# Second mixer: the rotation taken from the projection itself, head scales applied last; a fourth chunk by seven products in the last down projection

## The chip, the cores and the metric

The program runs on one core of one Trainium2 chip. The metric is the device time of one execution in microseconds (us). The kernel before has a median of 954.87 us over three executions (954.74 to 955.77).

A core has five instruction streams that run beside one another and meet through semaphores. PE (TensorE) multiplies matrices, and loads its stationary operand in instructions of their own (PEld). DVE (VectorE) and ACT (ScalarE) work element by element and can read the matrix results in PSUM. POOL (GpSimd) works element by element, on SBUF. SP (SyncE) issues most of the transfers. Each stream is executed in the order in which the program was written.

## The reference, cut to what matters

Two layers, each with two half-step feed-forward networks around a mixer. Sequence 256, width 1024, all in float32.

```python
for i in range(DEPTH):
    h = rmsnorm(x, ffn1_norm[i])
    x = x + 0.5 * swiglu(h, ffn1_w_gate[i], ffn1_w_up[i], ffn1_w_down[i])
    h = rmsnorm(x, mix_norm[i])
    q_s, k_s, v_s, q_m = jnp.split(h @ w_in[i], [768, 1536, 2304], axis=-1)
    ...                                   # memory attention o_m, both layers
    if i % 2 == 0:
        ...                               # first mixer: chunked attention with a bias
    else:                                 # second mixer
        q = rmsnorm(q_s.reshape(B, S, 6, 2, 64), b_q_norm[j])
        k = rmsnorm(k_s.reshape(B, S, 6, 2, 64), b_k_norm[j])
        q = apply_rope(q, cos, sin)
        k = apply_rope(k, cos, sin)
        ...                               # differential attention o_s
    x = x + jnp.concatenate([o_s, o_m], axis=-1) @ w_out[i]
    h = rmsnorm(x, ffn2_norm[i])
    x = x + 0.5 * swiglu(h, ffn2_w_gate[i], ffn2_w_up[i], ffn2_w_down[i])
```

`apply_rope` turns the two halves of each head of 64 by an angle: `[x1 cos - x2 sin, x2 cos + x1 sin]`. The norm multiplies a head by one number, and the rotation is linear, so the two can change places as long as the gains of the norm are folded into the tables of cosines and sines, which they are.

## The kernel before

**Products in three.** Every matrix product of weights and activations is taken in float32 by splitting both sides into a high part (rounded to the type fp32r) and a low part, the rest. `dense` (L504) issues three matmuls of 128x512 for one block: high times high (L511), high times low weights (L514), low activations times high weights (L517). One block is 128 rows of a weight matrix by 512 columns.

**Weights.** All weights stream through once. A "chunk" is 1 MB of weights, four blocks. `loader` brings chunks into three buffers `raw`, over SP's queue. `split_hi` (ACT, L338) casts each block to `hi`, and `split_lo` (DVE, L356) subtracts to get `lo`. Four buffers of `hi` and four of `lo` hold split chunks. A raw buffer is free again when the last `lo` of its chunk is done, and a split buffer when PE has used it.

**Chunks by seven.** In a down projection a chunk has a 2x2 form: two halves of the inner dimension and two of the columns, and the two token blocks make it two by two on the other side as well. A plain chunk takes 8 blocks of PE (`down`, four weight blocks for two token blocks each). A chunk by seven (`seven_item`, `seven_forms`, `seven`, `seven_sums`) takes 7, in the manner of Strassen and Winograd: it makes four sums of weight blocks (`wsum`, L350), splits seven blocks instead of four, makes four sums of activation blocks (`sf`, L681), splits those as well (L690, L694), and gathers four of its products in PSUM banks `m`, which `seven_sums` adds to the result once, behind the last such chunk. `SEVEN` (L377) lists for each feed-forward network which of the 11 chunks go by seven. The first of a list takes two split buffers. The others are "guests": one split buffer, and for the blocks 4 to 6 the tiles `xh` and `xl` of the activations, which are idle during the down projection (`gxh`, `gxl`). Only one guest can be in them: `xt_room` is set at the start of the down projection and again when PE has used a guest up, and the next guest is not split before. The activation side of the third and later chunk of a list waits until PE has reached the second chunk of the list (`prog[0] >= sv[1]`). The last three chunks, 8 to 10, come last for each quarter of the result.

**The order.** All streams are written in one order, made when the program is built. `Flow` (L47) is a small clock: each step says how long it takes on its engine (`flow.act`, `flow.dve`, `flow.pool`), and each thread of work, a Python generator, is resumed when the clock says that what it waits for is done. PE's stream is the backbone; work of other threads is put between its blocks when the clock has it ready. A step that takes longer on the chip than its line says is therefore put too early in PE's stream, and PE waits for it there.

**The second mixer.** `proj` runs five projections: heads 0 to 3 of q and k, v, then the two other groups of q and k, and the rest of v with the memory's q. `qk_evac` takes each result `pj` (128 tokens by 512, 8 heads) through `head_norm`: square on ACT (L916), sum by head on DVE (L919), scale and add on DVE (L530) and power -1/2 on POOL (L532), then the product of the result and both scales on DVE (L925, `qkn`). Then the rotation: two products with the sines on POOL (L1259), one with the cosines on DVE (L1262), their sum on DVE (L1266). Then four transposes on PE (`qktp`, L525), and copies to `qk`, `k` and `q`. There are six such chains, three groups by two token blocks. `attn_diff` follows for each. ACT also copies attention weights out of PSUM (L1374), and `of` (L1512) is a scale of the attention's own norm, which also has a power on POOL.

Of the kernel before, what the change touches and what calls it, by code (L numbers as in the profile page):

```python
# [12 lines left out]
F32 = mybir.dt.float32  # L13
# [3 lines left out]
AF = mybir.ActivationFunctionType  # L17
ALU = mybir.AluOpType
AX = mybir.AxisListType

P = 128
# [3 lines left out]
HD = 64  # L25
# [3 lines left out]
EPS = 1e-6  # L29
# [113 lines left out]
def kernel(  # L143
# [10 lines left out]
    nc = tc.nc  # L154
    PSUM = bass.MemoryType.PSUM
    NRAW, NHL, NT2 = 3, 4, 19
    flow = Flow()
# [11 lines left out]
    banks = Slots(flow, pp, "ps", 8)  # L169
    g4 = Slots(flow, gp, "g", 12)  # L170
    g2 = Slots(flow, t2, "t", NT2)
    ctx.enter_context(tc.manual_schedule())

    def small(shape, name):
        return sm.tile(shape, F32, tag="s", name=name)
# [18 lines left out]
    nhalf = const.tile([P, 8], F32, name="nhalf")  # L194
# [179 lines left out]
    def rows2(w, r):  # L374
        return [(lambda raw: k2(raw), w[r * 256:(r + 1) * 256, :].rearrange("(k p) n -> p k n", p=P))]

    SEVEN = {(0, 1): (), (0, 2): (1, 4, 7), (1, 1): (1, 4, 7), (1, 2): (1, 4, 7)}  # L377
    PAIR = {(0, 1): 4, (0, 2): 3, (1, 1): 3, (1, 2): 3}

    def turned2(w, r):  # L380
# [147 lines left out]
    def rsqrt(dst, ss, n, scale):  # L528
        v = small([P, 8], "v")
        nc.vector.tensor_scalar(out=v[:, :n], in0=ss, scalar1=scale, scalar2=EPS, op0=ALU.mult, op1=ALU.add)  # L530
        yield flow.dve(n)
        nc.gpsimd.tensor_tensor(out=dst, in0=v[:, :n], in1=nhalf[:, :n], op=ALU.pow)  # L532
        yield flow.pool(0.3 + 0.165 * n)


    class Xt:
# [81 lines left out]
    def ffn(l, nm, xt, gc_next):  # L618
        hts = [None] * NG
        htt = [None] * NG  # L620
        sv = SEVEN[l, nm]
        prog = [-1]
# [290 lines left out]
    def head_norm(ps, nh, rstd, name):  # L913
        yield g2.has(4)
        sq = g2.take([P, nh * HD], F32, "sq")
        nc.scalar.activation(sq, ps, AF.Square, scale=rstd)  # L916
        yield flow.act(nh * HD)
        ss = small([P, 8], "hss")
        nc.vector.tensor_reduce(out=ss[:, :nh], in_=sq.rearrange("p (h d) -> p h d", d=HD), axis=AX.X, op=ALU.add)  # L919
        g2.give()  # L920
        flow.dve(nh * HD)
        f = small([P, 8], "hf")
        yield from rsqrt(f[:, :nh], ss[:, :nh], nh, 1.0 / HD)
        nat = g2.take([P, nh * HD], F32, name)
        nc.vector.scalar_tensor_tensor(out=nat.rearrange("p (h d) -> p h d", d=HD),  # L925
                                       in0=ps.rearrange("p (h d) -> p h d", d=HD), scalar=rstd,
                                       in1=f[:, :nh].unsqueeze(2).broadcast_to([P, nh, HD]),
                                       op0=ALU.mult, op1=ALU.mult)
        yield flow.dve(nh * HD, 0.06)
        return nat  # L930
# [160 lines left out]
    ropeC = const.tile([P, 2, 2, HD], F32, name="ropeC")  # L1091
    ropeS = const.tile([P, 2, 2, HD], F32, name="ropeS")
# [109 lines left out]
    def mixer(l, xt, gc_next):  # L1202
        typ_a = l % 2 == 0
# [33 lines left out]
        class Heads:  # L1237
            def __init__(self):
                self.t = [None, None]
                self.k = None  # L1240

        def qk_evac(c):
            def run(ps, tb, t):
                qk = qkt.setdefault(c, Heads())
                yield t
                yield lambda: xt.rt[tb] is not None
                nat = yield from head_norm(ps, 8, xt.r[tb], "qkn")
                banks.give()
                if not typ_a:
                    yield g2.has(2)  # L1250
                    n4 = nat.rearrange("p (j h d) -> p j h d", j=2, h=4)
                    m2 = g2.take([P, 512], F32, "m2")
                    m1 = g2.take([P, 512], F32, "m1")
                    m1v = m1.rearrange("p (j h d) -> p j h d", j=2, h=4)
                    m2v = m2.rearrange("p (j h d) -> p j h d", j=2, h=4)
                    for hf in range(2):
                        own = slice(hf * 32, hf * 32 + 32)
                        oth = slice(32 - hf * 32, 64 - hf * 32)
                        nc.gpsimd.tensor_tensor(  # L1259
                            out=m2v[:, :, :, own], in0=n4[:, :, :, oth],  # L1260
                            in1=ropeS[:, tb, :, own].unsqueeze(2).broadcast_to([P, 2, 4, 32]), op=ALU.mult)
                    nc.vector.tensor_tensor(out=m1v, in0=n4,  # L1262
                                            in1=ropeC[:, tb].unsqueeze(2).broadcast_to([P, 2, 4, HD]), op=ALU.mult)
                    flow.dve(512)
                    yield flow.pool(1.4)
                    nc.vector.tensor_add(m1, m1, m2)  # L1266
                    g2.give(2)
                    nat = m1
                    yield flow.dve(512)
                yield banks.has()  # L1270
                tp = bank("qktp")
                for j in range(4):
                    t = turn(tp[:, j, :], nat[:, j * P:(j + 1) * P], typ_a and j < 2)
                g2.give()
                yield t
                gq, gk = (gcs[:, 2:3], gcol[:, GC_AK:GC_AK + 1]) if typ_a else (None, None)
                ts_ = slice(tb * P, (tb + 1) * P)
                yield lambda: g2.left > 0 and (g4.left > 0 if tb == 0 else qk.k is not None)
                if tb == 0:
                    qk.k = g4.take([P, 2, 2, SEQ], F32R, f"k{c}")  # L1280
                    qk.f = f = g2.take([P, 2, 2, P], F32, f"qk{c}")
                    if typ_a:
                        nc.scalar.activation(f[:, 0], tp[:, 0:2, :], AF.Copy, scale=gq)
                        nc.scalar.activation(f[:, 1], tp[:, 2:4, :], AF.Copy, scale=gk)
                        flow.act(256)
                        t = flow.act(256)
                    else:
                        nc.scalar.copy(out=f.rearrange("p a b c -> p (a b) c"), in_=tp)
                        t = flow.act(512)
                    banks.give()  # L1290
                    yield t
                    nc.scalar.copy(out=qk.k[:, 0, :, ts_], in_=f[:, 1])
                    yield flow.act(256)
                    nc.vector.tensor_sub(qk.k[:, 1, :, ts_], f[:, 1], qk.k[:, 0, :, ts_].bitcast(F32))
                    flow.dve(256)
                else:
                    qk.q = g2.take([P, 2, 2, P], F32R, f"q{c}")
                    yield from split_evac((qk.k[:, 0, :, ts_], qk.k[:, 1, :, ts_]), tp[:, 2:4, :], gk)
                    t = yield from split_evac((qk.q[:, 0], qk.q[:, 1]), tp[:, 0:2, :], gq)
                    banks.give()  # L1300
                qk.t[tb] = t
            return run
# [308 lines left out]
        for tb in range(2):  # L1611
            flow.spawn(finish(acc, tb, nxt, gc_next, False))
            for hf in range(2):
                for i in range(2, 4):
                    for k in range(2):
                        t = outp(i, k, tb, hf)
# [10 lines left out]
    xt = Xt(PAIR[0, 1] is not None)  # L1627
# [34 lines left out]
    for l in range(DEPTH):  # L1662
        xt = ffn(l, 1, xt, GC_MIX + l * KT)
        xt = mixer(l, xt, GC_FFN2 + l * KT)
        xt = ffn(l, 2, xt, None if l == DEPTH - 1 else GC_FFN1 + (l + 1) * KT)
# [53 lines left out]
```

## Time and profile before

| | us |
|---|---|
| median of three executions | 954.87 |
| the profiled execution, whole | 955.69 |
| its span, first to last instruction | 953.9 |
| PE busy | 945.6 |
| DVE busy | 820.0 |
| ACT busy | 587.0 |
| POOL busy | 109.1 |

The profile counts a matmul as busy from start to end, and matmuls overlap: one of 128x512 is shown as 0.39 us long, and the next starts after 0.23 us. What a matmul costs is therefore read from the distance of the starts. The granted clock of PE is full all through the execution. The second mixer lies between about 670 and 765 us of the span; the last down projection lies between 892 and 950 us.

### The profile page before, as it was taken

The page shows a single profiled execution, that of the slowest core. Times are in us where ns is not written, and L with a number is a line of the kernel's source. Part 1 is how long each engine was busy: PE and PEld are TensorE (multiplying, and loading weights), DVE is VectorE, ACT ScalarE, POOL GpSimd, SP SyncE. Part 2 cuts the span into 40 slices and gives each one's busy share as a digit, 9 for nine tenths or more (in the row PEclk, how much of TensorE's full clock was granted, in tenths as well). Part 3 has the DMA queues.
Part 4 walks back from the last instruction along what each step waited for, and adds up shares of the span by engine and source line. Part 5 has one row for each costly group of instructions (what it writes and reads, how often), then busy time and mean ns, then how long its engine had stood idle before and what let it go on. Part 6 is the DMA issues. An engine that isn't in the chain of part 4 may idle for free.

```text
span 953.9 us, 13334 instructions
## 1 busy us (share of the span) xinstructions
PE 945.6 (99%) x4475; PEld 774.1 (81%) x4475; DVE 820.0 (86%) x1483; ACT 587.0 (62%) x1121; POOL 109.1 (11%) x160
## 2 busy tenths in 40 slices
PE   9999999999999999999999999999999999999998
PEld 7888888887777888888888888888787778888886
DVE  7898978888777899979889899796999888999884
ACT  6556566677676746647546656564676865665650
POOL 1000057621210100000000000000434200000000
PEclk9999999999999999999999999999999999999999
DMA  8987799486525387887746679775641367588751
GB/s 265 289 263 236 224 354 296 158 276 210 177 90 177 97 266 225 262 287 219 245 146 219 208 226 288 247 253 166 196 158 57 121 214 228 183 275 276 239 197 45
DMA packets 169887, 204.04 MB, mean 214 GB/s; under 512 B 10137, under 2 KB 145114, under 8 KB 169818
## 3 DMA queue, kind: packets, MB, share of 16 engines
q1 hardware_dynamic: 169498, 202.78, 66.0%
q8 instruction: 35, 0.57, 0.3%
q10 hardware_dynamic: 320, 0.40, 0.1%
q14 instruction: 34, 0.28, 0.1%
HBM read 188.99 MB, written 14.16 MB: 213 GB/s over the span
## 4 chain that ended last, share of the span: by engine, by line
PE 90%; DVE 6%; DMA 2%; ACT 1%; issue 1%; SPq 0%; ACTq 0%; DVEq 0%
PE gu L517 13%; PE gu L514 13%; PE gu L511 13%; PE acc L511 9%; PE acc L517 9%; PE acc L514 9%; PE pair_m L511 3%; PE pair_m L514 3%; PE pair_m L517 3%; PE pj L517 2%; PE pj L511 2%; PE pj L514 2%; DVE lo L356 2%; PE S L1360 1%; DMA x<-in_x_dram 1%; PE AV L1441 1%
## 5 line engine op out<-in xcount | busy, mean ns | idle before, releaser
L338 ACT CAST hi<-raw 128x512 fp32r<-128x512 f32 (+1 forms) x467 | 336.3, 770 | 172.6 <-DMA raw<-in_ffn_w_up_dram 45.6
L356 DVE TENSOR_TENSOR lo<-raw,hi 128x512 fp32r<-128x512 f32 (+1 forms) x467 | 391.9, 875 | 35.5 <-ACT hi L338 35.4
L514 PE MATMUL gu<-lo,xh 128*128 128x512 f32 x576 | 224.7, 390 | 0.5 <-DVE lo L356 0.5
L517 PE MATMUL gu<-hi,xl 128*128 128x512 f32 x576 | 224.5, 390 | 0.4 <-DVE xl L562 0.4
L511 PE MATMUL gu<-hi,xh 128*128 128x512 f32 x576 | 224.4, 390 | 0.0
L517 PEld LDWEIGHTS gu<-hi,xl 128*128 128x128 f32 x576 | 108.1, 188 | 23.9 <-DVE xl L562 1.7
L514 PEld LDWEIGHTS gu<-lo,xh 128*128 128x128 f32 x576 | 108.1, 188 | 23.5 <-DVE lo L356 1.4
L511 PEld LDWEIGHTS gu<-hi,xh 128*128 128x128 f32 x576 | 108.2, 188 | 22.3
L517 PE MATMUL acc<-hi,ht 128*128 128x512 f32 x280 | 109.5, 391 | 0.0
L511 PE MATMUL acc<-hi,ht 128*128 128x512 f32 x280 | 109.2, 390 | 0.0
L514 PE MATMUL acc<-lo,ht 128*128 128x512 f32 x280 | 109.1, 390 | 0.0
L338 ACT CAST hi<-wsum 128x512 fp32r<-128x512 f32 x82 | 47.7, 619 | 26.5 <-DVE wsum L350 26.5
L514 PE MATMUL pj<-lo,xh 128*128 128x512 f32 x160 | 64.0, 400 | 0.0
L517 PE MATMUL pj<-hi,xl 128*128 128x512 f32 x160 | 63.8, 399 | 0.0
L511 PE MATMUL pj<-hi,xh 128*128 128x512 f32 x160 | 63.8, 399 | 0.0
L514 PEld LDWEIGHTS acc<-lo,ht 128*128 128x128 f32 x280 | 52.6, 188 | 10.9
L517 PEld LDWEIGHTS acc<-hi,ht 128*128 128x128 f32 x280 | 52.6, 188 | 10.8
L511 PEld LDWEIGHTS acc<-hi,ht 128*128 128x128 f32 x280 | 52.6, 188 | 10.7
L532 POOL TENSOR_TENSOR xr<-v,nhalf 128x1 f32<-128x1 f32 x12 | 10.3, 861 | 435.1 <-DVE v L530 435.1
L356 DVE TENSOR_TENSOR lo<-wsum,hi 128x512 fp32r<-128x512 f32 x82 | 52.8, 680 | 0.0
L633 ACT ACTIVATE sil<-gu,xr 128x256 f32<-128x256 f32 x72 | 33.7, 468 | 29.8 <-PE gu L517 29.7
L532 POOL TENSOR_TENSOR hf<-v,nhalf 128x8 f32<-128x8 f32 (+1 forms) x20 | 31.4, 1570 | 87.3 <-DVE v L530 78.9
(232 smaller groups left out, 1429.5 us busy)
## 6 DMA issues: line engine op xcount, KB each, us to landing
raw<-in_ffn_w_down_dram SPq DMA_DIRECT2D x176, 256.0 KB, 4.5
raw<-in_ffn_w_gate_dram SPq DMA_DIRECT2D x82, 512.0 KB, 4.0
raw<-in_ffn_w_up_dram SPq DMA_DIRECT2D x82, 512.0 KB, 5.4
raw<-in_w_in_dram SPq DMA_DIRECT2D x32, 512.0 KB, 4.4
hd<-hb SPq DMA_DIRECT2D x44, 256.0 KB, 4.6
hr<-hd SPq DMA_DIRECT2D x44, 256.0 KB, 4.6
raw<-in_w_out_dram SPq DMA_DIRECT2D x8, 1024.0 KB, 5.1
raw<-in_w_mem_kv_dram SPq DMA_DIRECT2D x4, 1024.0 KB, 5.3
```

The source lines that it names most:

```text
L338: nc.scalar.copy(out=it.part(0, q, w), in_=src())
L356: nc.vector.tensor_sub(it.part(1, q, w), src(), it.part(0, q, w).bitcast(F32))
L511: nc.tensor.matmul(out=ps, lhsT=xh, rhs=wh, start=start, stop=False)
L514: nc.tensor.matmul(out=ps, lhsT=xh, rhs=wl, start=False, stop=False)
L517: nc.tensor.matmul(out=ps, lhsT=xl, rhs=wh, start=False, stop=stop)
L532: nc.gpsimd.tensor_tensor(out=dst, in0=v[:, :n], in1=nhalf[:, :n], op=ALU.pow)
L633: nc.scalar.activation(sil, ps[tb][:, 0:256], AF.Silu, scale=xt.r[tb])
L1360: nc.tensor.matmul(out=ss[e][:, pr, :nk], lhsT=q[rows, pr, :], rhs=k[rows, pr, :], start=i == 0, stop=i == len(passes) - 1)
L1441: nc.tensor.matmul(out=av[64 * e:64 * e + 64, pr, :], lhsT=vsrc(kb, pr, e), rhs=pts[e][:, pr, kb, :], start=(kb == 0), stop=(kb == nb - 1))
```

## The change

There are three edits.

1. In the second mixer the rotation no longer waits for the norm. A copy of the projection goes to SBUF on ACT (`own`), ahead of the square. DVE multiplies the projection in PSUM by the cosines, after which the PSUM bank is given back; POOL multiplies the copy by the sines, the two halves crossed. The sum of squares and its power run beside that, with the power behind the two products in POOL's stream. DVE adds the two products, and a last DVE step multiplies by the token's scale and the head's scale. The first mixer keeps `head_norm`.
2. The clock's lines: the power on POOL is taken as 0.5 + 0.17 n us for n columns in place of 0.3 + 0.165 n, everywhere (`rsqrt`); the two products on POOL as 2.1 us in place of 1.4, and the power inside the new function as 1.9 us.
3. In the last down projection the chunks by seven are 1, 3, 5 and 7 in place of 1, 4 and 7.

```diff
-    SEVEN = {(0, 1): (), (0, 2): (1, 4, 7), (1, 1): (1, 4, 7), (1, 2): (1, 4, 7)}
+    SEVEN = {(0, 1): (), (0, 2): (1, 4, 7), (1, 1): (1, 4, 7), (1, 2): (1, 3, 5, 7)}
...
         nc.gpsimd.tensor_tensor(out=dst, in0=v[:, :n], in1=nhalf[:, :n], op=ALU.pow)
-        yield flow.pool(0.3 + 0.165 * n)
+        yield flow.pool(0.5 + 0.17 * n)
...
+        def rotated(ps, tb, rstd):
+
+            heads = lambda t: t.rearrange("p (j h d) -> p j h d", j=2, h=4)
+            yield g2.has(4)
+            own, sq, m1, m2 = (g2.take([P, 512], F32, n) for n in ("qko", "sq", "m1", "m2"))
+            nc.scalar.copy(out=own, in_=ps)
+            ta = flow.act(512)
+            nc.scalar.activation(sq, ps, AF.Square, scale=rstd)
+            ts = flow.act(512)
+            nc.vector.tensor_tensor(out=heads(m1), in0=heads(ps),
+                                    in1=ropeC[:, tb].unsqueeze(2).broadcast_to([P, 2, 4, HD]), op=ALU.mult)
+            t = flow.dve(512)
+            banks.give()
+            yield ta
+            for hf in range(2):
+                to = slice(hf * 32, hf * 32 + 32)
+                src = slice(32 - hf * 32, 64 - hf * 32)
+                nc.gpsimd.tensor_tensor(out=heads(m2)[:, :, :, to], in0=heads(own)[:, :, :, src],
+                                        in1=ropeS[:, tb, :, to].unsqueeze(2).broadcast_to([P, 2, 4, 32]), op=ALU.mult)
+            tm = flow.pool(2.1)
+            yield max(t, ts)
+            ss = small([P, 8], "hss")
+            nc.vector.tensor_reduce(out=ss, in_=sq.rearrange("p (h d) -> p h d", d=HD), axis=AX.X, op=ALU.add)
+            g2.give()
+            flow.dve(512)
+            f, v = small([P, 8], "hf"), small([P, 8], "v")
+            nc.vector.tensor_scalar(out=v, in0=ss, scalar1=1.0 / HD, scalar2=EPS, op0=ALU.mult, op1=ALU.add)
+            yield flow.dve(8)
+            nc.gpsimd.tensor_tensor(out=f, in0=v, in1=nhalf, op=ALU.pow)
+            tf = flow.pool(1.9)
+            yield tm
+            nc.vector.tensor_add(m1, m1, m2)
+            g2.give(2)
+            flow.dve(512)
+            yield tf
+            by_head = lambda t: t.rearrange("p (h d) -> p h d", d=HD)
+            nc.vector.scalar_tensor_tensor(out=by_head(m1), in0=by_head(m1), scalar=rstd,
+                                           in1=f.unsqueeze(2).broadcast_to([P, 8, HD]), op0=ALU.mult, op1=ALU.mult)
+            yield flow.dve(512, 0.1)
+            return m1
...
-                nat = yield from head_norm(ps, 8, xt.r[tb], "qkn")
-                banks.give()
-                if not typ_a:
-                    yield g2.has(2)
-                    n4 = nat.rearrange("p (j h d) -> p j h d", j=2, h=4)
-                    m2 = g2.take([P, 512], F32, "m2")
-                    m1 = g2.take([P, 512], F32, "m1")
...
-                    for hf in range(2):
...
-                        nc.gpsimd.tensor_tensor(
-                            out=m2v[:, :, :, own], in0=n4[:, :, :, oth],
-                            in1=ropeS[:, tb, :, own].unsqueeze(2).broadcast_to([P, 2, 4, 32]), op=ALU.mult)
-                    nc.vector.tensor_tensor(out=m1v, in0=n4,
-                                            in1=ropeC[:, tb].unsqueeze(2).broadcast_to([P, 2, 4, HD]), op=ALU.mult)
-                    flow.dve(512)
-                    yield flow.pool(1.4)
-                    nc.vector.tensor_add(m1, m1, m2)
-                    g2.give(2)
-                    nat = m1
-                    yield flow.dve(512)
+                if typ_a:
+                    nat = yield from head_norm(ps, 8, xt.r[tb], "qkn")
+                    banks.give()
+                else:
+                    nat = yield from rotated(ps, tb, xt.r[tb])
```

## What was predicted

> **What bounds the kernel now.** I read the page first: the busy shares and the chain of waits.
>
> ```profile
> span 953.9 us, 13334 instructions
> ...
> PE 945.6 (99%) x4475; PEld 774.1 (81%) x4475; DVE 820.0 (86%) x1483; ACT 587.0 (62%) x1121; POOL 109.1 (11%) x160
> ...
> PE 90%; DVE 6%; DMA 2%; ACT 1%; issue 1%; SPq 0%; ACTq 0%; DVEq 0%
> ```
>
> PE is never idle for long. So time goes down in two ways only: fewer matmuls, or shorter gaps between them. The second view, PE's waits from 660 to 790 us, holds the second mixer and the entry of the last feed-forward network; the third gives the stages' busy time.
>
> ```profile
> PE qktp L525 <- DVE m L1266: 0.7, 2, 0.6
> PE otp L525 <- DVE of L1512: 0.5, 1, 0.5
> PE AV L1498 <- ACT PT L1374: 0.5, 1, 0.5
> PE gu L517 <- DVE xl L562: 0.4, 1, 0.4
> ```
> ```profile
> 670.00:760.00 90.00, 88.03 (x487) 69.78 (x487) 82.60 (x184) 64.60 (x180) 32.60 (x27) 1.00 0.42 137
> 893.00:932.00 39.00, 39.00 (x174) 32.30 (x173) 35.19 (x64) 25.20 (x49) 0.00 (x0) 1.00 0.61 200
> ```
>
> The columns of the last two rows are the stretch, its length, then busy us of PE, PEld, DVE, ACT and POOL, the granted clock (1.00) and DMA. In the mixer all of PE's waits make 0.7 + 0.5 + 0.5 = 1.7 us, and the entry behind it 0.4. Only the first row, 0.7 us, belongs to the rotation. DVE is the next engine, 82.6 of 90 us, but it mostly runs ahead of PE. In the last down projection PE has no gap at all, so there only a smaller number of matmuls helps.
>
> **The fourth chunk by seven.** One block less is three matmuls less. What they cost is the distance of starts, since each is shown as 0.39 us and overlaps the next:
>
> ```profile
> 914.02 0.39 PE L511 MATMUL acc<-hi,h 128*128 128x512 f32 x1
> 914.25 0.39 PE L514 MATMUL acc<-lo,h 128*128 128x512 f32 x1
> 914.47 0.39 PE L517 MATMUL acc<-hi,h 128*128 128x512 f32 x1
> 914.70 0.39 PE L511 MATMUL acc<-hi,h 128*128 128x512 f32 x1
> ```
>
> From 914.02 to 914.70 is 0.68 us for three. **-0.68 us**, if the blocks arrive in time. What is added is DVE and ACT work, and these rows price it:
>
> ```profile
> 898.60 2.50 DVE L356 TENSOR_TENSOR lo<-raw,hi 128x512 fp32r<-128x512 f32 x4 [0.77 <-ACT hi L338]
> ...
> 902.34 0.68 DVE L350 TENSOR_TENSOR wsum<-raw 128x512 f32<-128x512 f32 x1
> 902.94 0.68 DVE L350 TENSOR_TENSOR wsum<-raw,wsum 128x512 f32<-128x512 f32 x1
> ...
> 913.18 0.28 DVE L681 TENSOR_TENSOR sf<-hr 128x128 f32<-128x128 f32 x1
> ...
> 914.11 0.69 DVE L350 TENSOR_TENSOR wsum<-raw 128x512 f32<-128x512 f32 x1
> ...
> 929.88 2.50 DVE L356 TENSOR_TENSOR lo<-raw,hi 128x512 fp32r<-128x512 f32 x4 [2.94 <-ACT hi L338]
> ```
>
> A step of 512 columns starts 0.60 us behind the one before. Three more `lo` (1.8), four `wsum` (2.4) and four `sf` (913.18 to 914.11, 0.93), and `lo` of the activations in three pieces in place of one, which I estimate from the same rows at +0.5: DVE gets 5.6 us more. It has 39.0 - 35.2 = 3.8 us idle there, nearly all of it the two waits of 0.77 and 2.94 us for `hi`. So 1.8 us don't fit and eat the lead. How large is the lead? Chunk 10's four `lo` end at 929.88 + 2.50 = 932.4. The last part begins where the guest ends:
>
> ```profile
> 933.06 0.39 PE L511 MATMUL acc<-gxh,h 128*128 128x512 f32 x1
> ...
> 933.74 0.39 PE L511 MATMUL acc<-hi,ht 128*128 128x512 f32 x1
> ```
>
> Chunk 10 is the fifth block from 933.74, at 933.74 + 4 x 0.68 = 936.5. The lead is 4 us; with 1.8 us of overload and PE 0.68 us earlier 1.5 are left. The guests follow closer (5 behind 3, 7 behind 5, one plain chunk of 8 x 0.68 = 5.5 us between). A guest's blocks 4 to 6 need three casts and three `lo` behind its forerunner's end, under 4 us, and are used 5.5 + 4 x 0.68 = 8.2 us behind it: covered. ACT gets about 2.3 us (three casts and two small steps) and is busy 25 of 39. Transfers don't grow: SP brings the same chunks, and three raw buffers free later by up to the 1.8 us. If the cover fails, PE waits for a `lo`: up to 1.8 us, so this edit lies between -0.7 and +1.1. I take -0.68, since every lead found is larger than the overload.
>
> **The rotation.** What each chain uses now, from the grouped rows:
>
> ```profile
> L916 ACT ACTIVATE sq<-pj,xr 128x512 f32<-128x512 f32 x12 | 8.3, 688 | 1.6 <-PE pj L517 1.5
> L925 DVE SCALAR_TENSOR_TENSOR qkn<-pj,xr,hf 128x512 f32<-128x512 f32 x12 | 8.9, 744 | 0.3 <-POOL hf L532 0.3
> L1374 ACT COPY PT<-ptp 128x512 f32<-128x512 f32 x17 | 9.8, 584 | 3.6 <-PE ptp L525 3.4
> L1259 POOL TENSOR_TENSOR m<-qkn,ropeS 128x256 f32<-128x256 f32 x12 | 12.1, 1027 | 7.5 <-DVE qkn L925 4.7 <-ACT k L1022 1.8 <-PE pj L517 1.1
> L532 POOL TENSOR_TENSOR hf<-v,nhalf 128x8 f32<-128x8 f32 x6 | 11.0, 1832 | 17.4 <-DVE v L530 9.1 <-DVE sst L583 8.3
> ```
>
> DVE: sum, scale, two products, one addition before; the same five after, so I put DVE at 0 (one product changes from SBUF to PSUM input, the head scales the other way). ACT: six copies more, 6 x 0.58 = 3.5 us, hidden in ACT's 25 us of idle time. POOL: the same instructions. PE: the same.
>
> The chain in length: before, square 0.69, sum 0.69, scale 0.17, power 1.83, product 0.74, two POOL products 2.05, addition 0.68: 6.9 us without queues. After: copy 0.58, POOL products 2.05, power 1.83 behind them, last product 0.74 (as L925, its nearest row; 0.68 as other DVE steps at least): 5.2 us; the branch through square and sum is done earlier. 1.7 us shorter, but PE has other blocks meanwhile, so the length itself is worth nothing. What counts is whether the clock's places fit.
>
> ```profile
> 685.19 0.39 PE L517 MATMUL pj<-hi,xl 128*128 128x512 f32 x1
> 686.15 0.63 PE L525 MATMUL qktp<-ident,m 128*128 128x128 f32 x4 [0.57 <-DVE m L1266]
> ...
> 691.24 0.63 PE L525 MATMUL qktp<-ident,m 128*128 128x128 f32 x4 [0.16 <-DVE m L1266]
> ```
>
> These are the two waits for the rotated result. The clock's 1.4 us for POOL's products stands against 2.05 measured, and 0.3 + 0.165 x 8 = 1.62 for the power against 1.83: 0.64 us too early in all, the size of the larger wait. The new lines, 2.1 and 1.9, fit. So I take these **-0.7 us** as gained. The wait for `of` has the same reason (0.63 on the clock for n = 2, 0.84 after the change); I credit half of its 0.5, **-0.2**. The other waits I leave as they are: the first mixer and other stages also get the new power lines, but wait for nothing now.
>
> Against it stands the new copy at the head of the chain, in ACT's queue:
>
> ```profile
> 674.80 0.69 ACT L916 ACTIVATE sq<-pj,xr 128x512 f32<-128x512 f32 x1 [0.52 <-PE pj L517]
> ...
> 681.59 1.67 ACT L338 CAST hi<-raw 128x512 fp32r<-128x512 f32 x3 [1.95 <-DMA raw<-in_w_in_dram]
> 683.16 0.68 ACT L916 ACTIVATE sq<-pj,xr 128x512 f32<-128x512 f32 x1
> ```
>
> The first token block's projection ended by 674.8, the second's 24 matmuls of 0.227 later, at about 680.0. Its square began at 683.16 only: three casts stood ahead, and the first waited 1.95 us for a transfer. In the new kernel the copy stands there. From 683.16 the new chain takes 5.2 to 5.9 us (0.7 for queues and hops), to 688.4 to 689.1. On the clock it takes some 6.5 us from 680.0; PE runs about 5% slower than the clock's 0.216 us, so the transposes stand at about 686.9. A wait of 1.5 to 2.2 us, if the transfer is as late as now; before, a longer chain with more queues on the clock hid most of it (0.16 us remained). DVE's queues on the clock may hide it again, as they did: 0 to 2.2 us. I take **+0.5**, nearer to the row of 0.16.
>
> [...]
>
> ```profile
> L1262 DVE TENSOR_TENSOR m<-qkn,ropeC x6: 678/954/1235, 681.2 to 729.6; 128x512 f32<-128x512 f32 x6
> ...
> 709.60 1.23 DVE L356 TENSOR_TENSOR lo<-raw,hi 128x512 fp32r<-128x512 f32 x1
> ```
>
> The product with the cosines takes 0.68 or 1.23 us, and a `lo` beside POOL's products 1.23 as well: 0.55 us lost on DVE each time. [...]
>
> **Sum.** -0.68 - 0.7 - 0.2 + 0.5 = -1.1 us. Against the profiled execution, 955.69 us (span 953.9 and 1.8 around it), that is 954.6. That execution lies 0.8 above the median of 954.87, so for the median I say **953.8**. A measurement of this kernel can tell about 0.2%, 1.9 us, from no change.
>
> **Rivals.**
> *All the mixer's waits go* (chance 0.25). The shorter chain and the truer clock also take away the waits for `of` and PT and the one behind (0.4): 1.7 + 0.4 + 0.68 = -2.8 us, 952.1. For it: three of the four wait for steps whose clock lines are too short. Against: PT's copy isn't touched.
> *The late copy* (0.10), the other side. Each chain's first step is now behind ACT's casts, and power and products share POOL. If the first case costs 2.2 us and the four chains behind it each 0.57, as at 686.15, that is +4.5, less 0.7 and 0.68: +3.1 us, 958.0. It decides from the point at which a copy starts more than 1.3 us (6.5 x 1.05 less 5.5) behind its projection's end. For it: the 3.2 us at 683.16. Against: only that one square was so late.
> *The last stage gains nothing* (0.12). DVE's 1.8 us show up on PE: -0.68 + 1.8, less 0.4 in the mixer: +0.7, 955.6. For it: DVE at 35 of 39. Against: the lead of 4 us.
> *The change does nothing in the mixer* (0.08): the waits only change their places, -0.68: 954.2.
> The forecast has 0.45.
>
> **How the numbers follow.** Faster by over 0.2% (under 952.96) is the first rival: 0.25. Slower by over 0.2% is the late copy: 0.10. The rest, 0.65, lies within. The range takes in the first rival and the last stage's loss with part of the late copy: 951.8 to 956.6.
>
> **What would show it.** Right: PE's three matmuls fewer and no gap from 893 to 950; no wait `qktp <- m` but at most one, near 687 to 689; the copy near 683. Wrong: PE waits in the last down projection, waits for `lo` in the mixer, or a mixer whose waits go wholly.

## The result and the profile after

The changed kernel is slower, by half a per cent. Each ratio below is that of the kernel to the one before, measured beside it on the same chip; it is worked out over all executions and differs from the quotient of the two medians by up to 0.07%.

| | changed | before, beside it |
|---|---|---|
| median, us | 960.33 (6 executions) | 955.34 (6 executions) |
| lowest and highest, us | 958.25 to 962.28 | 954.74 to 956.53 |
| ratio, 95% interval | 1.0051 (1.0034 to 1.0067) | |
| profiled execution, whole, us | 959.48 | 955.69 |
| its span, us | 957.7 | 953.9 |

So 5.0 us were lost where 1 us of gain was forecast, and the time lies outside the range. These are the lines of the page after that answer to those shown of before: the span, the busy times, and the shares of the chain of waits.

```profile
span 957.7 us, 13357 instructions
...
PE 945.7 (99%) x4472; PEld 774.8 (81%) x4472; DVE 821.1 (86%) x1496; ACT 591.2 (62%) x1132; POOL 104.5 (11%) x160
...
PE 90%; DVE 3%; DMA 3%; ACT 3%; issue 0%; SPq 0%; POOL 0%; ACTq 0%; DVEq 0%; POOLq 0%
```

The page does not show the loss at first sight: DVE's work grew by 1.1 us only, and its share of the chain fell. PE's busy time is the same to 0.1 us although three matmuls are gone. The stages tell more. The largest of PE's waits from 670 to 790 us, and below them the largest of DVE's from 670 to 760 us (line that waits, what it waited for, us in total, times, longest):

```profile
PE qktp L525 <- DVE m L1278: 3.0, 3, 1.6
PE AV L1521 <- ACT PT L1397: 0.7, 1, 0.7
PE otp L525 <- ACT pe L1431: 0.3, 1, 0.3
```
```profile
DVE m L1251 <- ACT sq L1249: 7.5, 6, 2.3
```

The wait for the rotated result did not go: it grew from 0.7 to 3.0 us. And DVE has a wait that the kernel before had no counterpart of. L1251 is the product with the cosines, which reads the projection in PSUM. It waits for ACT's square (L1249), **whose result it does not use**, six times in six chains, 7.5 us in all. The largest wait of DVE in this stretch was 2.0 us before:

```profile
DVE nm L1400 <- PE S L1360: 2.0, 1, 2.0
DVE hss L919 <- ACT sq L916: 1.5, 1, 1.5
```

The dearest case is at 726 to 731 us. First DVE, then POOL, then ACT, each in its timeline after the change (start, us, engine, line, operation, operands; idle time before it and its releaser in brackets):

```profile
724.16 0.68 DVE L1273 TENSOR_TENSOR m<-m,m 128x512 f32<-128x512 f32 x1
...
725.09 0.68 DVE L356 TENSOR_TENSOR lo<-raw,hi 128x512 fp32r<-128x512 f32 x1
728.11 0.69 DVE L1251 TENSOR_TENSOR m<-pj,ropeC 128x512 f32<-128x512 f32 x1 [2.34 <-ACT sq L1249]
728.72 0.81 DVE L1278 SCALAR_TENSOR_TENSOR m<-m,xr,hf 128x512 f32<-128x512 f32 x1
```
```profile
723.01 1.64 POOL L1270 TENSOR_TENSOR hf<-v,nhalf 128x8 f32<-128x8 f32 x1 [2.03 <-DVE rs L1502]
```
```profile
724.55 2.18 ACT L338 CAST hi<-raw 128x512 fp32r<-128x512 f32 x4
726.63 0.37 ACT L1397 COPY PT<-ptp 128x256 f32<-128x256 f32 x1
726.89 0.59 ACT L1247 COPY qko<-pj 128x512 f32<-128x512 f32 x1
727.37 0.71 ACT L1249 ACTIVATE sq<-pj,xr 128x512 f32<-128x512 f32 x1
```

The last step of the fifth chain (L1278 at 728.72) needs POOL's power, done at 723.01 + 1.64 = 724.65, and the addition, done at 724.16 + 0.68 = 724.84. But the sixth chain's cosine product stands ahead of it in DVE's stream, and that starts at 728.11, 0.03 us behind the end of the square (727.37 + 0.71 = 728.08). So a step that had been ready for some 4 us stood in line: for the first 0.9 us behind two other DVE steps, then behind one that waited for ACT's queue of four casts, two copies and the square. PE's timeline over the same stretch:

```profile
727.05 0.71 PE L1521 MATMUL AV<-V,PT 128*128 128x128 f32 x4 [0.68 <-ACT PT L1397]
727.52 0.48 PE L514 MATMUL pj<-lo,xh 128*128 128x512 f32 x1
729.58 0.66 PE L525 MATMUL qktp<-ident,m 128*128 128x128 f32 x4 [1.58 <-DVE m L1278]
730.00 0.61 PE L517 MATMUL pj<-hi,xl 128*128 128x512 f32 x1
730.40 0.63 PE L511 MATMUL pj<-hi,xh 128*128 128x512 f32 x1
...
733.39 0.49 PE L514 MATMUL pj<-lo,xh 128*128 128x512 f32 x1
```

PE waits 1.58 us for that step. Its two other waits for a rotated result, 0.52 us at 692 and 0.93 us at 719, come 6 to 7 us behind such a halt of DVE (0.75 us at 685, 1.54 us at 711), and DVE has no gap in between in which it could catch up. After the longest wait the matmuls start 0.42 us apart up to 733.39: eight distances of 0.424 us in place of 0.227, 1.6 us, as much again as the wait. The windows show the clock (stretch, its length, busy us of PE, PEld, DVE, ACT and POOL with counts, granted clock, DMA share, GB/s):

```profile
893.00:932.00 39.00, 39.00 (x174) 32.31 (x173) 38.20 (x73) 27.24 (x54) 0.00 (x0) 1.00 0.60 193
726.00:729.50 3.50, 1.32 (x13) 0.80 (x9) 1.39 (x2) 3.41 (x10) 1.42 (x2) 1.00 0.17 67
729.50:733.50 4.00, 3.92 (x13) 3.14 (x14) 3.86 (x11) 2.82 (x11) 2.12 (x2) 0.59 0.00 0
```

From 726.0 to 729.5 PE worked for 1.32 of 3.5 us, and in the 4 us behind it the granted clock was 0.59; before the change it was 1.00 throughout. The first of the three rows is the last down projection: no idle time of PE in 39 us, with DVE at 38.2.

Where the 3.8 us between the two profiled spans lie can be read from the starts of PE's matmuls with the same number in the two traces: the changed kernel is 0.7 us behind at 15 us, 1.6 when the second mixer begins, 5.6 within it at 730 us (the order differs there), 4.5 at its end, 3.8 at the end of all. So the second mixer made 2.9 net, the last stage gave 0.7 back, and the first 1.6 came ahead of any step whose code changed but for the clock's lines. Those 1.6 us arise at two places. At the start PE waits 1.5 us for the input in this execution and 0.3 in that of before. In the first mixer there is a wait of 0.76 us at 233 us that before has not, and it is as large in the first experiment below, whose order there is that of before. The rows are PE's waits from 5 to 20 us and PE's timeline after the change, then PE's waits from 220 to 240 us in the first experiment:

```profile
PE xtp L525 <- DMA x<-in_x_dram: 1.5, 2, 0.9
```
```profile
233.41 0.53 PE L525 MATMUL ptp<-flip,pe 128*128 128x128 f32 x2 [0.76 <-DVE pe L1445]
```
```profile
PE ptp L525 <- DVE pe L1422: 0.8, 1, 0.8
```

These are differences from one execution to another. So differences of about 1 us between single profiles prove nothing below; the ratios decide.

### The profile page after: what moved, and what is told of

Its sections match the earlier page's. It is cut to its first block, busy times and chain, and to the rows that moved or that the text cites. A ratio compares the mean times of both kernels' runs of the same rounds, so it can differ in the third digit from the quotient of the medians.

```text
span 957.7 us, 13357 instructions
## 1 busy us (share of the span) xinstructions
PE 945.7 (99%) x4472; PEld 774.8 (81%) x4472; DVE 821.1 (86%) x1496; ACT 591.2 (62%) x1132; POOL 104.5 (11%) x160
## 4 chain that ended last, share of the span: by engine, by line
PE 90%; DVE 3%; DMA 3%; ACT 3%; issue 0%; SPq 0%; POOL 0%; ACTq 0%; DVEq 0%; POOLq 0%
PE gu L514 14%; PE gu L511 14%; PE gu L517 14%; PE acc L511 9%; PE acc L517 9%; PE acc L514 9%; PE pj L517 3%; PE pair_m L511 3%; PE pair_m L514 3%; PE pair_m L517 3%; PE pj L514 3%; PE pj L511 3%; DVE lo L356 1%; ACT hi L338 1%; PE S L1383 1%; DMA x<-in_x_dram 1%
## 5 line engine op out<-in xcount | busy, mean ns | idle before, releaser
L517 PE MATMUL acc<-hi,ht 128*128 128x512 f32 x272 | 106.4, 391 | 0.0
L511 PE MATMUL acc<-hi,ht 128*128 128x512 f32 x272 | 106.1, 390 | 0.0
L514 PE MATMUL acc<-lo,ht 128*128 128x512 f32 x272 | 106.0, 390 | 0.0
L517 PEld LDWEIGHTS acc<-hi,ht 128*128 128x128 f32 x272 | 51.1, 188 | 10.5
L511 PEld LDWEIGHTS acc<-hi,ht 128*128 128x128 f32 x272 | 51.1, 188 | 10.3
L636 DVE SCALAR_TENSOR_TENSOR h<-gu,xr,sil 128x256 f32<-128x256 f32 x72 | 34.3, 476 | 7.0 <-ACT sil L633 6.9
```

The lines of the kernel that those rows point to most:

```text
L511: nc.tensor.matmul(out=ps, lhsT=xh, rhs=wh, start=start, stop=False)
L514: nc.tensor.matmul(out=ps, lhsT=xh, rhs=wl, start=False, stop=False)
L517: nc.tensor.matmul(out=ps, lhsT=xl, rhs=wh, start=False, stop=stop)
L636: nc.vector.scalar_tensor_tensor(out=h, in0=ps[tb][:, 256:512], scalar=xt.r[tb], in1=sil, op0=ALU.mult, op1=ALU.mult)
```

## The experiments

All kernels, with the median and the ratio to the kernel before. The letters are used below.

| | kernel | median, us | before, us | ratio (95%) |
|---|---|---|---|---|
| A | seven chunks alone | 955.19 | 955.91 | 0.9999 (0.9988 to 1.0009) |
| B | power line alone | 957.54 | 955.91 | 1.0022 (1.0010 to 1.0034) |
| C | rotation alone | 956.75 | 955.91 | 1.0009 (1.0000 to 1.0018) |
| D | changed, product written behind the square | 957.48 | 955.91 | 1.0012 (1.0002 to 1.0022) |
| E | the changed kernel again | 960.95 | 955.93 | 1.0052 (1.0037 to 1.0066) |
| F | changed, square reads the copy | 959.30 | 955.93 | 1.0037 (1.0023 to 1.0051) |
| G | changed, product reads the copy | 956.23 | 955.93 | 1.0003 (0.9988 to 1.0019) |
| H | D with the old power line | 957.15 | 955.93 | 1.0013 (1.0002 to 1.0024) |
| I | changed, PE kept busy at one wait | 960.41 | 956.09 | 1.0048 (1.0032 to 1.0063) |
| K | G with the old power line | 955.29 | 956.09 | 0.9990 (0.9981 to 0.9999) |
| L | product and square read the copy | 954.86 | 956.09 | 0.9990 (0.9981 to 0.9998) |
| M | L with the old power line | 954.95 | 955.52 | 0.9999 (0.9986 to 1.0013) |

The reading of above, by the starts of PE's matmuls, gives the time of the second mixer alone in each profiled execution. It is longer than before by 2.9 us in the changed kernel, 4.8 in E, 2.0 in F and 4.3 in I. In all the others it lies between -1.1 and +0.5 us. A, whose order is that of before up to the last stage, has the -1.1, so about 1 us of such a difference is chance. The loss, then, sits in the second mixer, and in those four kernels only.

**The theory** after the result: the cosine product does not start on the bank before ACT's copy and square are through with it (0.03 us behind the square, above), is written too early for that, and holds up DVE's stream. **Rivals:** the fourth chunk by seven overloads DVE; the new power line moves the whole order to a worse place; the copies in ACT's queue are simply late.

### One part of the change at a time: A, B, C

A, before with the new list only:

```diff
-    SEVEN = {..., (1, 2): (1, 4, 7)}
+    SEVEN = {..., (1, 2): (1, 3, 5, 7)}
```

> The kernel before with nothing but the new list of chunks by seven in the last down projection. Theory: this edit does what was worked out, three matmuls of 0.227 us less with no gap in the last down projection: -0.7 us, 954.6 to 954.9 beside a kernel before of about 955.3, and PE's time up to the last stage as before. Rival (the last stage pays): DVE's added 5.6 us show up as PE waits for lo there, and the time is 955.3 or more.

The time is that of before, within 0.1%. In the profile the stretch from the last feed-forward network to the end is 0.67 us shorter than before, and there is no wait of PE from 790 us on. So the fourth chunk does what it says and is not what loses time; 0.67 us are below what the interval can tell.

B, before with the power's new line only:

```diff
-        yield flow.pool(0.3 + 0.165 * n)
+        yield flow.pool(0.5 + 0.17 * n)
```

> The kernel before with nothing but the power's new line on the clock, 0.5 + 0.17 n. Theory (the lines are only truer): waits in both mixers stay as they are or shrink, 954.5 to 955.5. Rival (the line moves work to worse places): the wait of 0.75 us for pe in the first mixer, which the changed kernel shows at 232 us and the kernel before doesn't, is there: +0.7 to +1.0, 956 to 956.4.

2.1 us slower (0.22%). PE's waits from 670 to 790 us:

```profile
PE AV L1498 <- ACT PT L1374: 0.8, 1, 0.8
PE AV L1441 <- ACT PT L1374: 0.6, 2, 0.3
PE S L1360 <- DVE rs L1479: 0.4, 1, 0.4
PE otp L525 <- DVE qmT L1029: 0.4, 1, 0.4
```

The row for `qktp` is gone, as the prediction said of the new line. But it is gone in A as well, where the line is the old one and the order of this stage that of before, so B does not show that the line removed it. The waits of this stretch make 2.2 us, where they made 2.1 before, and the second mixer as a whole takes 0.4 us less than before in this execution. What is longer in it lies ahead of the mixer: 1.85 us, with a wait of 1.3 us for `pe` in the first mixer, the one that the rival named. Since A has 0.8 us of that wait without the line, one profile does not tell how much of B's 2.1 us it explains; where B's loss comes from stays open.

C, before with the new `rotated` only (list and power line of before):

> The kernel before with nothing but the new rotation in the second mixer. Theory (DVE held by the bank): DVE's product with the cosines waits each time until ACT is through with its copy and its square of the same PSUM bank, and DVE's queue stands meanwhile. Six such waits, 6 to 8 us of DVE in all, PE waits of 2 us or more for qktp, and a lower granted clock behind a long one: 957.5 to 961. Rival (the power's line or the start does it): 955 to 956, with PE waits for qktp under 1 us.

0.9 us slower, with an interval that begins at 1.0000: far less than the theory wanted, though the waits on the square are there. First the waits of the cosine product, then the largest of PE's from 670 to 790 us:

```profile
  ACT sq L1249: 6.1, 5
```
```profile
PE otp L525 <- DVE o L1537: 1.6, 2, 0.8
PE qktp L525 <- DVE m L1278: 0.9, 1, 0.9
```

6.1 us of idle DVE cost 0.9 us here, and the second mixer of this execution is no longer than before (-0.2 us). So DVE's idle time is not the price by itself; what stands behind the waiting product, and how soon PE needs it, should set the price. The order in DVE's stream supports that. In C the last step of the fifth chain (L1278) is written ahead of the sixth chain's cosine product, in the changed kernel behind it (728.72 against 728.11):

```profile
723.36 0.75 DVE L1278 SCALAR_TENSOR_TENSOR m<-m,xr,hf 128x512 f32<-128x512 f32 x1
725.32 0.69 DVE L1251 TENSOR_TENSOR m<-pj,ropeC 128x512 f32<-128x512 f32 x1 [1.21 <-ACT sq L1249]
```

PE does not wait for that step in C. No run varied this place alone. The three parts alone make -0.1, +2.1 and +0.9 us, 2.9 in all, against 5.0 together: they are not additive.

### The product moved: D, and the changed kernel again: E

D writes the product behind the square's time on the clock, so that it stands in DVE's stream where it can start:

```diff
-            nc.vector.tensor_tensor(out=heads(m1), in0=heads(ps), ...)
-            t = flow.dve(512)
-            banks.give()
             yield ta
...
-            yield max(t, ts)
+            yield ts
+            nc.vector.tensor_tensor(out=heads(m1), in0=heads(ps), ...)
+            flow.dve(512)
+            banks.give()
```

> The changed kernel with DVE's product with the cosines written only when the clock says that ACT's square is done, everything else as it is. Theory (DVE held by the bank): the product finds the bank free, DVE no longer stands in front of it (under 2 us in all in place of 7.5), PE's waits for qktp fall from 3.0 to under 1 us, the clock stays full: 954.5 to 956. Rival (the late copy): the copies start as late in ACT's queue as in the changed kernel, the chain from copy to last product is as long, and the waits for qktp stay at 2 us or more: 958 to 961.

> The changed kernel once more, beside the others on this chip. Every theory: 959.5 to 961.5 with a kernel before of about 956; in the profile DVE's product with the cosines starts 0.04 us behind the end of ACT's square each time. If the loss of the first profile at 726 to 733 us (1.58 us of PE idle, then 3.4 us of half clock) belongs to the order, a PE wait for qktp of over 1 us is there again; if it was chance, there is none and the time is 957 to 958.

E repeats the loss: 1.0052 beside 1.0051. D is lower by 0.39%, 3.7 us, and its interval (up to 1.0022) lies apart from E's (from 1.0037). It does not take back all: at 957.48 it is above the 954.5 to 956 of the theory, and its interval begins above 1. In D's profile the product waits for the square once, 0.8 us; the rows are DVE's of D, then the two largest of PE's of D, then the product's and PE's of E:

```profile
DVE m L1259 <- ACT sq L1249: 0.8, 1, 0.8
```
```profile
PE AV L1521 <- ACT PT L1397: 1.0, 1, 1.0
PE S L1383 <- ACT pe L1431: 0.7, 1, 0.7
```
```profile
  ACT sq L1249: 8.5, 6
```
```profile
PE qktp L525 <- DVE m L1278: 4.0, 3, 1.6
PE otp L525 <- ACT pe L1431: 1.2, 1, 1.2
```

In D no wait for `qktp` is left, though two of its copies start 2.46 and 1.41 us behind the end of their projections. In this order, late copies alone do not make PE wait. E's profile has the half clock as well (0.57 from 729.5 to 733.5 us), D's has not (1.00). One reservation: the clock that orders the streams reacts to the edit, so D's matmuls stand in another order than the changed kernel's from 684 to 785 us. D alone cannot separate the wait from the order.

### Which read is it: F and G

F lets the square read the copy in place of the bank, and leaves the order of all streams as it was (the two traces show the same sequence of instructions on each engine):

```diff
-            nc.scalar.activation(sq, ps, AF.Square, scale=rstd)
+            nc.scalar.activation(sq, own, AF.Square, scale=rstd)
```

> The changed kernel with ACT's square taken from the copy in SBUF in place of the projection in PSUM; all streams keep their order. Theory (DVE held by the bank): the product with the cosines now waits for the copy alone and starts 0.04 us behind the copy's end, 0.6 us earlier in each of the six chains; DVE's idle time in front of it falls from 7.5 to about 4 us, PE's waits for qktp from 3.0 to 1 to 2 us: 1 to 2 us faster than the changed kernel. Rival (the product waits for the square's result or for ACT's queue as such): it still starts behind the square's end, and the time is that of the changed kernel.

This is the sharpest test of what the product waits for. Its rows in F:

```profile
L1251 DVE TENSOR_TENSOR m<-pj,ropeC x6: 691/692/694, 677.0 to 727.1; 128x512 f32<-128x512 f32 x6
...
  ACT qko L1247: 4.1, 5
```

With the square out of the bank the product is released by **the copy's** end instead, the only other reader on ACT, whose result it does not use either. In all six chains it starts 0.03 us behind the copy's end, 0.7 to 0.8 us ahead of the square's. The idle time falls from 7.5 to 4.1 us, PE's for `qktp` from 3.0 to 2.2. So the wait follows the readers of the bank. The time falls by the 1 to 2 us expected, from 1.0052 (E, on the same chip) to 1.0037, but not beyond the intervals: the half clock is still there (0.64 from 729.5 to 733.5 us).

G takes the product out of the bank and writes it behind the copy:

```diff
-            nc.vector.tensor_tensor(out=heads(m1), in0=heads(ps), ...)
-            t = flow.dve(512)
-            banks.give()
             yield ta
+            nc.vector.tensor_tensor(out=heads(m1), in0=heads(own), ...)
+            t = flow.dve(512)
...
             yield max(t, ts)
+            banks.give()
```

> The changed kernel with the product with the cosines taken from the copy in SBUF, written when the clock says that the copy is done. Theory: no bank to wait for, DVE idle in front of it under 2 us in all, PE waits for qktp under 1 us, the time that of the kernel with the product behind the square, +0.5 to +2 us over the kernel before; the product has two SBUF inputs again and takes up to 1.23 us beside POOL's products. Rival (the late copy): PE's waits for qktp stay at 2 us or more, +4 us or more.

```profile
L1252 DVE TENSOR_TENSOR m<-qko,ropeC x6: 689/960/1227, 677.9 to 726.0; 128x512 f32<-128x512 f32 x6
...
  ACT qko L1247: 0.4, 1
```

G is not told from before (1.0003), 0.48% under the changed kernel, 4.6 us. Its order differs from the changed kernel's too. It pays another price: the product has two operands in SBUF now and takes 0.69 us in three chains and 1.23 in three, while from PSUM it took 0.69 in all six. Those three times 0.54 us are less than what the waits cost.

### The power line in other orders, and both reads moved: H, K, L, M

H, K and M are D, G and L with `flow.pool(0.3 + 0.165 * n)` in `rsqrt`; L is F and G together.

> The product behind the square, the four chunks by seven, and the power's old line 0.3 + 0.165 n on the clock in head_norm and the other norms. Theory (the power's line alone costs about 2 us, as the kernel with that edit alone showed): 1 to 2 us under the kernel with the line, 955 to 956, at or under the kernel before. Rival (what the line costs depends on the order around it): no gain over the kernel with the line, +1 to +2 us over the kernel before.

> The kernel with the product with the cosines taken from the copy, and the power's old line 0.3 + 0.165 n. Theory (what the power's line costs depends on the order around it): within 1 us of the kernel with the new line, 955.2 to 957. Rival (the line alone costs 2 us): 954 to 954.5 beside a kernel before of 955.9.

> The changed kernel with both the square and the product with the cosines taken from the copy, so that the projection's bank is read once. Theory: as the kernel with the product from the copy, PE waits for qktp under 1 us, 955.5 to 956.5; nothing is left of the bank, so little more is to be had. Rival (the bank, held for ACT's second pass, still delays something): 1 us or more faster than that kernel, 954.5 to 955.3.

> Square and cosine product from the copy, four chunks by seven, the power's old line: what the runs so far point to as the fastest. Theory: the bank is out of the way and the last stage has its 0.7 us: 1 to 1.5 us under the kernel before, a ratio of 0.9985 to 0.999. Rival (the two gains of 1 us seen alone are one and the same, or an effect of the order): no better than the kernel before, 0.9995 to 1.001.

The new line makes -0.0001 in the ratio from H to D, +0.0013 from K to G and -0.0009 from M to L: none is outside the intervals, and the signs differ. H therefore misses its theory, which expected 1 to 2 us from the old line, and the rival holds: what the line costs depends on the order around it. L is 1.2 us under G, nearer to its rival than to its theory, but the intervals overlap. M was written as what should be fastest, 1 to 1.5 us under before, and is not told from before, as its rival said.

K and L are 0.1% under before, about 1 us, with intervals that end at 0.9999 and 0.9998. But they are the best two of four kernels of one kind, and G (1.0003) and M (0.9999) show no gain. So with the reads apart the change is worth between nothing and 1 us; a gain is not shown.

These runs bear on the reservation about the order. Six kernels in which the product no longer stands in front of the bank (D, G, H, K, L, M) have four different orders of PE's matmuls, and all lie at 1.0013 or below. The four with the product in front and the changed kernel's order (the changed kernel, E, F, I) lie at 1.0037 to 1.0052. C, with the product in front in another order, lies at 1.0009. C differs from the changed kernel in the norms' power line and the list of chunks only, and the list costs nothing in A. So the loss takes two things together: a product that waits at the bank, and the order that the new line makes, in which a step that PE needs soon stands behind it. Without either of them at most 0.13% is left.

### Is it the half clock: I

I is the changed kernel with six matmuls of 128x128 ahead of the fifth chain's transposes, which PE can do while it waits; nothing reads their result. The trace shows each as two.

```diff
             tp = bank("qktp")
+            if not typ_a and (c, tb) == (2, 0):
+                for j in range(6):
+                    nc.tensor.matmul(out=tp[:, j % 4, :], lhsT=ident, rhs=ident, start=True, stop=True)
```

> The changed kernel with six more matmuls of 128x128 (the identity by itself, about 0.21 us each) into the bank of the fifth chain's transposes, just ahead of them, where PE stood idle for 1.6 us. They compute nothing that is used. Theory of the clock (PE's idle time before it lowers the granted clock): the six take 1.3 us of time in which PE would have waited anyway, the wait shrinks by as much, the 3.4 us at half clock behind it are gone in the profile, and the kernel is 1 to 1.8 us faster than the changed kernel, 959 to 960, although it does more. Rival (the low clock comes from elsewhere, or at random): the half clock stays, and the time is that of the changed kernel or up to 1.3 us more.

PE's timeline and the window behind it, then PE's waits from 670 to 790 us, in I:

```profile
728.68 1.50 PE L1297 MATMUL qktp<-ident 128*128 128x128 f32 x12
730.42 0.66 PE L525 MATMUL qktp<-ident,m 128*128 128x128 f32 x4 [0.24 <-DVE m L1278]
```
```profile
730.00:735.00 5.00, 4.76 (x24) 3.69 (x22) 4.86 (x12) 3.75 (x14) 2.59 (x2) 1.00 0.00 0
```
```profile
PE qktp L525 <- DVE m L1278: 2.5, 3, 1.4
PE AV L1524 <- ACT PT L1400: 2.2, 2, 1.5
PE otp L525 <- ACT pe L1434: 0.8, 1, 0.8
```

In this profile the clock stays at 1.00, as the theory said. The time is not the 1 to 1.8 us shorter that it said (1.0048 against 1.0052 and 1.0051), and the second mixer takes 4.3 us more than before at full clock. PE's other waits are larger than in the changed kernel, 2.2 us for PT in place of 0.7.

All executions together settle more. 3.4 us at half clock in 957.7 make a mean granted clock of 0.998. Four of the twelve executions of the changed kernel (the result and E) have a mean of 1.000, which leaves no room for that stretch, and they took 958.25, 958.81, 961.09 and 962.52 us, beside medians before of 955.34 and 955.93. They lie 2.9 to 6.6 us above those, so most of the loss is there without the half clock. The other eight have a median of 961.0; what the half clock adds is not told from the spread.

## Why the prediction was wrong

**The step that failed** is the one on DVE: "sum, scale, two products, one addition before; the same five after, so I put DVE at 0", with the product with the cosines taken to run beside ACT's copy and square. The count was right, and the product from PSUM takes 0.69 us. What failed is "beside". DVE's product and ACT's two steps read one PSUM bank, and the trace shows the product released by the end of ACT's last read in all six chains (F: of the copy, when that is the last): 7.5 us of idle DVE, a wait that the sum put at nothing. The change's own clock leaves it out as well: `flow.dve(512)` counts the product at once, without waiting for ACT. Since the product is written first in DVE's stream, everything behind it waits too. The prediction asked of the *transposes* what would be late next, but not of the *new reader* what it would have to wait for and who is queued behind it. D and G, which move that one product (and with it the order), are 3.7 and 4.6 us faster, of the 5.0 us lost. What a given wait costs depends on the order: C has 6.1 us of the same waits and loses 0.9.

DVE's work itself was not 0 either: in C its busy time falls from 820.0 to 815.5 us. One part of that is the cosine product, which reads the projection in PSUM: the six took 5.7 us before and take 4.2 now.

The traces show the order of these reads and its price: the product starts 0.03 us behind the square's end, six times of six, with 7.5 us of idle DVE. In the changed kernel's trace each of the six products waits for the semaphore that ACT's copy and square raise, so the order is in the built program; what happens without it no run here shows.

**The truer clock removes the waits for the rotated result, -0.7.** In the changed kernel these waits grew to 3.0 us. In B the row is gone, but in A too, so it can go by chance, and no run shows the line removing it. Nor was the clock truer. The lines 2.1 and 1.9 were fitted to what POOL's steps took in the kernel before, 2.05 and 1.83 us. In the changed kernel the two products take 2 x 0.74 us and the power 1.64 us in the median (shortest, median and longest, in ns):

```profile
L1259 POOL TENSOR_TENSOR m<-qko,ropeS x12: 724/738/743, 677.0 to 728.3; 128x256 f32<-128x256 f32 x12
...
L1270 POOL TENSOR_TENSOR hf<-v,nhalf x6: 1637/1644/2057, 680.5 to 731.4; 128x8 f32<-128x8 f32 x6
```

The old lines, 1.4 and 1.62, would have fitted these. A duration read before a change is no safe input for a clock after it. And a line on the clock shuffles the whole order: the norms' line made 2.1 us in B and nothing that can be told in H, K and M, and it is, but for the list of chunks, all that lies between C (1.0009) and the changed kernel (1.0051), about 4 us. So this term had the wrong sign.

**Half of the wait for `of`, -0.2.** That row is gone, but 0.7 for PT and 0.3 for `pe` stand in the stage, where PT had 0.5: nothing gained.

**The late copy, +0.5, and the rival of 958.0.** The second chain's copy starts at 683.88 (the prediction said near 683), 2.13 us behind its projection's end; two more are 2.2 and 2.4 us late, one 0.6. Yet in D two copies are beyond the rival's point of 1.3 us, and no wait for `qktp` follows. The rival came nearest to the measured time, but its mechanism, PE waiting for the copy's own chain, is not what runs showed: a late copy hurt through the cosine product, which waited for the square behind it and kept DVE's stream waiting. That a rival at 958.0 came near was luck.

**Six copies hidden in ACT's idle time.** Right as to ACT's own load: its busy time grew from 587.0 to 591.2 us, the six copies and the last stage's casts. But what is queued on ACT now delays DVE, by the bank.

**The fourth chunk by seven, -0.68.** Right: no gap of PE from 893 to 950 us, the same 0.7 us in the starts, here and in A. DVE's busy time in A is 825.7 us in place of 820.0, 5.7 more where 5.6 were counted; in the window shown it is 38.2 of 39 us. The lead was enough.

## What to carry to other kernels

Before a second engine is let read a PSUM bank, count the readers of that bank: in the changed kernel and in F DVE's product came behind ACT's reads of it (by 0.03 us in all six chains), and the later step has to be written where it can start, or it holds up all that its engine does next. If the data is copied to SBUF anyway, let the second reader use the copy, and price the slower operation (in G 1.23 us in place of 0.69 for three of six products) against the wait (7.5 us of DVE in the changed kernel, 0.4 in G). And ask of each new instruction not only what it costs and whom it feeds, but whom it stands in front of.

## What the hardware showed that was not expected

**Two readers of one bank did not run at once.** Six of six products started 0.03 us behind the end of ACT's square, and 0.03 us behind the copy when the square had moved. The order is set by a semaphore in the program; these runs do not show what the chip would do without it.

**The clock halved behind short gaps, in some executions.** In the changed kernel's profile the granted clock is 0.50 from 730.2 to 733.6 us, and the distance of 512-column matmuls rises from 0.227 to 0.424 us there. From 729.5 to 733.5 us the clock is 0.57 in E's profile and 0.64 in F's. PE was not idle all the time ahead of that: from 726.0 to 729.5 us it was busy for 1.32 of 3.5 us in the changed kernel (gaps of 0.68 and 1.58 us) and for 1.22 in E, and from 725.0 to 728.5 us for 1.88 in F (gaps of 0.74 and 0.93 us). With six small matmuls in the larger gap the clock of I's profile stayed full (1.00 from 726 to 740 us). But four of the twelve executions of the changed kernel have a mean clock of 1.000 without them, and five of six of I, so part of it is chance. What lowers the clock these runs do not show.

**POOL's products were slower in the kernel before.** Each took 0.72 to 0.74 us in the changed kernel, where DVE waited or was in the product from PSUM for most of that time, and 0.73 to 1.27 in the kernel before. There the slowest, at 709.0 us, ran beside a `lo` that took 1.23 us in place of 0.68.

**The start of a run varies by about 1 us.** PE's wait for the input was 1.5 us in one execution and 0.3 in another, and a wait of 0.8 us in the first mixer came and went in kernels with the same order there. A reached the second mixer 1.0 us later than before, with the same order.
